# A re-planned start of a matmul kernel: load order, weight pieces and early next tiles

## The chip, the cores and the metric

The kernel runs on one core of a Trainium2 chip. Times are device microseconds of a whole execution. A profile shows one execution; its span, from the first to the last instruction, lies some 2 us under that execution's time (387.9 against 389.72 us for the kernel before).

## The reference

```python
# x: (8, 1024, 768) f32, w_qkv: (768, 2304) f32, out: (8, 1024, 2304) f32
rms = np.sqrt(np.mean(x ** 2, axis=-1, keepdims=True) + eps)
return np.matmul(x / rms * gamma, w_qkv)
```

## The kernel before

The 8,192 rows make 64 tiles of 128. A tile is converted to bf16, transposed (K onto the partitions), multiplied with the weights (six K blocks, columns in chunks of 512 and a last 256), scaled by 1/rms while the results are copied out of PSUM, the memory that TensorE writes to (an eviction), and stored. Gamma is multiplied into the weights as they are converted. Each engine runs its instructions in the order in which the plan lists them, and SyncE issues nearly all DMAs, also in that order.

Six tiles, the head, are planned by hand while the 7.1 MB of weights arrive. Each entry of the list has a planned time, which only sorts it; tiles 0 to 2 are transposed on TensorE in f32 in two parts (`trA`, `trB`), tiles 3 to 5 in bf16 (`tr`), all later ones by DMA.

```python
ARRIVALS = "xxxwwwxwwwwwxxwww"          # order of the first loads
PIECES = [(0, 1, 0, 512), (1, 2, 0, 512), ...]   # K blocks from, to; column, columns
HEAD_PLAN = [(4.41, "trA", 0), ..., (8.02, "mm", 0, 0, "0"), ...]   # cut
HEAD_END = 44.51
...
for t in range(HEAD, MT):
    at(now - 15, load_x, t)
    at(now - 8.5, cast, t)
    at(now - 7.5, trans_dma, t)
    at(now - 5, stat, t)
    at(now - 3, recip, t)
    for n0 in range(0, N, NT):
        at(now, mm, t, n0, range(KO))
        now += min(NT, N - n0) * US
        flip ^= 1
        evac_at(now + 0.2, t, n0, "DVE" if flip else "ACT", gap=1.2)   # and store
for _, _, fn, args in sorted(plan, key=lambda p: p[:2]):
    fn(*args)
```

Of the kernel before, what the change touches and what calls it, by code (L numbers as in the profile page):

```python
# [7 lines left out]



ARRIVALS = "xxxwwwxwwwwwxxwww"
PIECES = [(0, 1, 0, 512), (1, 2, 0, 512), (2, 3, 0, 512), (3, 4, 0, 512), (4, 5, 0, 512), (5, 6, 0, 512), (0, 3, 512, 512), (3, 6, 512, 512), (0, 6, 1024, 512), (0, 6, 1536, 512), (0, 6, 2048, 256)]

EARLY = 3


HEAD_PLAN = [
    (4.41, "trA", 0), (4.45, "stat", 0), (5.28, "trB", 0), (5.42, "cpA", 0, "DVE"),
    (5.71, "trA", 1), (5.85, "cpB", 0, "ACT"), (6.10, "recip", 0), (6.44, "stat", 2),
    (6.59, "trB", 1), (6.73, "cpA", 1, "DVE"), (6.80, "trA", 2), (7.11, "conv", 0, 0, "POOL"),  # L20
    (7.24, "trB", 2), (7.41, "cpB", 1, "DVE"), (7.77, "cpA", 2, "ACT"),
    (7.81, "conv", 1, 1, "DVE"), (8.02, "mm", 0, 0, "0"), (8.23, "mm", 1, 0, "0"),
    (8.29, "recip", 2), (8.39, "cpB", 2, "ACT"), (8.45, "conv", 2, 2, "DVE"),
    (8.45, "mm", 2, 0, "0"), (8.66, "mm", 0, 0, "1"), (8.75, "stat", 1), (8.88, "mm", 1, 0, "1"),
    (9.10, "mm", 2, 0, "1"), (9.31, "mm", 0, 0, "2"), (9.44, "cast", 3, "DVE"),
    (9.53, "mm", 1, 0, "2"), (9.74, "mm", 2, 0, "2"), (10.05, "tr", 3), (10.08, "stat", 3),
    (10.11, "conv", 3, 3, "DVE"), (10.59, "recip", 1), (10.65, "mm", 0, 0, "3"),
    (10.78, "conv", 4, 4, "DVE"), (10.87, "mm", 1, 0, "3"), (11.09, "mm", 2, 0, "3"),
    (11.26, "cp", 3, "DVE"), (11.32, "mm", 0, 0, "4"), (11.45, "conv", 5, 5, "ACT"),
    (11.54, "mm", 1, 0, "4"), (11.76, "mm", 2, 0, "4"), (11.82, "recip", 3),  # L30
    (11.97, "mm", 3, 0, "01234"), (13.05, "mm", 0, 0, "5"), (13.27, "mm", 1, 0, "5"),
    (13.47, "conv", 6, 0, "DVE"), (13.47, "conv", 6, 1, "ACT"), (13.47, "conv", 6, 2, "POOL"),
    (13.48, "mm", 2, 0, "5"), (13.70, "mm", 3, 0, "5"), (13.95, "evac", 2, 0, "DVE"),
    (14.01, "mm", 0, 512, "0"), (14.18, "evac", 0, 0, "ACT"), (14.22, "mm", 1, 512, "0"),
    (14.44, "mm", 0, 512, "12"), (14.70, "evac", 1, 0, "DVE"), (14.87, "evac", 3, 0, "ACT"),
    (14.87, "mm", 1, 512, "12"), (15.30, "mm", 2, 512, "012"), (15.48, "conv", 7, 4, "DVE"),
    (15.48, "conv", 7, 5, "POOL"), (15.95, "mm", 3, 512, "012"), (16.33, "conv", 7, 3, "POOL"),
    (16.47, "cast", 4, "DVE"), (16.47, "stat", 4), (16.60, "mm", 0, 512, "45"),
    (17.03, "mm", 1, 512, "4"), (17.24, "tr", 4), (17.47, "cast", 5, "DVE"),
    (17.58, "mm", 0, 512, "3"), (17.79, "mm", 1, 512, "35"), (17.80, "stat", 5),  # L40
    (18.02, "cp", 4, "DVE"), (18.23, "tr", 5), (18.56, "mm", 2, 512, "345"), (18.58, "recip", 4),
    (18.74, "evac", 1, 512, "DVE"), (19.13, "evac", 0, 512, "ACT"), (19.21, "mm", 3, 512, "345"),
    (19.49, "evac", 2, 512, "DVE"), (19.86, "mm", 4, 0, "012345"), (20.02, "evac", 3, 512, "ACT"),
    (20.24, "recip", 5), (20.40, "cp", 5, "DVE"), (21.15, "mm", 4, 512, "012345"),
    (21.49, "conv", 8, 2, "DVE"), (21.49, "conv", 8, 3, "ACT"), (21.97, "conv", 8, 0, "DVE"),
    (22.20, "conv", 8, 4, "ACT"), (22.45, "mm", 5, 0, "012345"), (22.45, "evac", 4, 0, "DVE"),
    (22.91, "evac", 4, 512, "ACT"), (23.60, "conv", 8, 1, "ACT"), (23.74, "mm", 5, 512, "012345"),
    (23.90, "evac", 5, 0, "DVE"), (24.31, "conv", 8, 5, "ACT"), (25.04, "mm", 0, 1024, "012345"),
    (25.20, "evac", 5, 512, "DVE"), (25.51, "conv", 9, 0, "POOL"), (25.51, "conv", 9, 1, "ACT"),
    (25.95, "conv", 9, 5, "DVE"), (26.33, "mm", 1, 1024, "012345"), (26.43, "conv", 9, 4, "DVE"),  # L50
    (26.49, "evac", 0, 1024, "ACT"), (26.91, "conv", 9, 2, "DVE"), (27.39, "conv", 9, 3, "DVE"),
    (27.63, "mm", 2, 1024, "012345"), (27.87, "evac", 1, 1024, "DVE"),
    (27.90, "conv", 10, 0, "POOL"), (27.90, "conv", 10, 2, "ACT"), (28.38, "conv", 10, 3, "ACT"),
    (28.62, "conv", 10, 5, "DVE"), (28.86, "conv", 10, 4, "ACT"), (28.92, "conv", 10, 1, "DVE"),
    (28.92, "mm", 3, 1024, "012345"), (29.22, "evac", 2, 1024, "DVE"),
    (30.22, "mm", 4, 1024, "012345"), (30.38, "evac", 3, 1024, "DVE"),
    (31.51, "mm", 5, 1024, "012345"), (31.67, "evac", 4, 1024, "DVE"),
    (32.81, "mm", 0, 1536, "012345"), (32.97, "evac", 5, 1024, "DVE"),
    (34.10, "mm", 1, 1536, "012345"), (34.26, "evac", 0, 1536, "DVE"),
    (35.39, "mm", 2, 1536, "012345"), (35.55, "evac", 1, 1536, "DVE"),  # L60
    (36.69, "mm", 3, 1536, "012345"), (36.85, "evac", 2, 1536, "DVE"),
    (37.98, "mm", 4, 1536, "012345"), (38.14, "evac", 3, 1536, "DVE"),
    (39.28, "mm", 5, 1536, "012345"), (39.44, "evac", 4, 1536, "DVE"),
    (40.57, "mm", 0, 2048, "012345"), (40.73, "evac", 5, 1536, "DVE"),
    (41.23, "mm", 1, 2048, "012345"), (41.39, "evac", 0, 2048, "ACT"),
    (41.88, "mm", 2, 2048, "012345"), (42.04, "evac", 1, 2048, "DVE"),
    (42.54, "mm", 3, 2048, "012345"), (42.70, "evac", 2, 2048, "DVE"),
    (43.19, "mm", 4, 2048, "012345"), (43.35, "evac", 3, 2048, "DVE"),
    (43.85, "mm", 5, 2048, "012345"), (44.01, "evac", 4, 2048, "DVE"),
    (44.67, "evac", 5, 2048, "DVE"),  # L70
]
HEAD_END = 44.51


@with_exitstack
def kernel(
# [20 lines left out]
    KO = K // P  # L97
    MT = M // P
    NT = 512
    HEAD = ARRIVALS.count("x")  # L100
    inv_k = 1.0 / float(K)
    PIECE_BUFS = {(k1 - k0, n): sum((q[1] - q[0], q[3]) == (k1 - k0, n) for q in PIECES)
                  for k0, k1, _, n in PIECES}

    PARTS = [(0, 1024), (1024, 1024), (2048, N - 2048)]

    singles = ctx.enter_context(tc.tile_pool(name="singles", bufs=1))
    wst = ctx.enter_context(tc.tile_pool(name="wst", bufs=3))
    xin = ctx.enter_context(tc.tile_pool(name="xin", bufs=8))
    stats = ctx.enter_context(tc.tile_pool(name="stats", bufs=12))  # L110
    junk = ctx.enter_context(tc.tile_pool(name="junk", bufs=2))
    xbp = ctx.enter_context(tc.tile_pool(name="xbp", bufs=4))
    xTp = ctx.enter_context(tc.tile_pool(name="xTp", bufs=HEAD + 3))
    outp = ctx.enter_context(tc.tile_pool(name="outp", bufs=7))
    psum = ctx.enter_context(tc.tile_pool(name="psum", bufs=8, space=bass.MemoryType.PSUM))

# [25 lines left out]
    def load_w(c):  # L142
        k0, k1, n0, n = PIECES[c]
        WF[c] = wst.tile([P, k1 - k0, n], f32, name=f"w_f{k1 - k0}_{n}", bufs=PIECE_BUFS[k1 - k0, n])
# [56 lines left out]
            XT[t] = xTp.tile([P, KO, P], bf16, name="xT")  # L201
        copy(eng, XT[t][:, slice(*HALF[h]), :], PT[t, h])

    def trans_dma(t):
        XT[t] = xTp.tile([P, KO, P], bf16, name="xT")
        nc.sync.dma_start_transpose(out=XT[t], in_=XB[t])

# [34 lines left out]
    def at(time, fn, *args):  # L242
        plan.append((time, len(plan), fn, args))
# [21 lines left out]
            nc.tensor.matmul(out=wps, lhsT=warm, rhs=warm, start=True, stop=True)  # L265


    nx = nw = 0
    for n, kind in enumerate(ARRIVALS):
        if kind == "x":  # L270
            at(0.1 * n - 9, load_x, nx)
            nx += 1
        else:
            at(0.1 * n - 9, load_w, nw)
            nw += 1
    at(0.0, idle, 30)
    ops = {"conv": conv, "cast": cast, "stat": stat, "recip": recip, "tr": tr, "cp": cp, "mm": mm}
    for time, op, *args in HEAD_PLAN:
        if op == "evac":
            evac_at(time, *args, gap=1.0)  # L280
        elif op[-1] in "AB":
            at(time, tr_half if op[:2] == "tr" else cp_half, args[0], op[-1], *args[1:])
        else:
            if op == "mm":
                args[2] = [int(k) for k in args[2]]
            at(time, ops[op], *args)
        if op == "trA" and args[0] == 0:
            at(time + 0.1, gamma_in)
        if op == "trB" and args[0] == EARLY - 1:
            at(time + 0.1, idle, 5)  # L290


    US = 6 * 0.2158 / 512
    now, flip = HEAD_END, 0
    for t in range(HEAD, MT):
        at(now - 15, load_x, t)
        at(now - 8.5, cast, t)
        at(now - 7.5, trans_dma, t)
        at(now - 5, stat, t)
        at(now - 3, recip, t)  # L300
        for n0 in range(0, N, NT):
# [3 lines that stand above are left out]
            evac_at(now + 0.2, t, n0, "DVE" if flip else "ACT", gap=1.2)  # L305
# [38 lines left out]
```

## Time and profile before

| | before |
|---|---|
| time, median | 389.93 us (389.67 to 390.10, 3 runs) |
| TensorE busy | 379.5 of 387.9 us |
| first product matmul | 8.48 us |
| tile 7's first matmul | 51.56 us, after a wait of 0.44 us |
| last eviction starts | 384.37 us |
| from there to the end (the tail) | 3.5 us |

TensorE is the limit from 8.5 us on.

### The profile page before, as it was taken

How to read it: one execution, taken by the hardware profiler on the slowest of the kernel's cores; microseconds unless marked ns; L12 is line 12 of the kernel's file. 1: busy time of each engine (PE TensorE's matmuls, PEld its weight loads, DVE VectorE, ACT ScalarE, POOL GpSimd, SP SyncE). 2: the span in 40 equal slices, each digit the busy share in tenths (PEclk: the TensorE clock that was granted, in tenths of full speed). 3: DMA queues.
4: the chain of work that ended last, by engine and by line, in shares of the span. 5: the costliest groups of instructions: out<-in, count | busy, mean ns of one | idle time of the engine just before them, and what ended most of it. 6: DMA issues, size and time to landing. Idle time of an engine off the chain costs nothing.

```text
span 387.9 us, 5500 instructions
## 1 busy us (share of the span) xinstructions
PE 379.5 (98%) x1953; PEld 194.3 (50%) x1992; DVE 159.1 (41%) x317; ACT 178.1 (46%) x359; POOL 5.9 (2%) x12
## 2 busy tenths in 40 slices
PE   7999999999999999999999999999999999999996
PEld 6444644554554554554554554554554554554553
DVE  3667634343433343433343433343334343334332
ACT  6652234544444544444534444534434535434532
POOL 1310000000000000000000000000000000000000
PEclk9999999999999999999999999999999999999999
DMA  7999999999999999999999999999999999999974
GB/s 272 392 384 358 308 369 284 397 301 274 333 311 305 279 326 295 290 330 300 276 346 288 302 317 280 318 311 304 287 318 301 297 318 303 287 325 292 292 264 189
DMA packets 87606, 119.51 MB, mean 308 GB/s; under 512 B 50710, under 2 KB 59676, under 8 KB 87580
## 3 DMA queue, kind: packets, MB, share of 16 engines
q1 hardware_dynamic: 87568, 119.17, 100.7%
q8 instruction: 15, 0.25, 0.3%
q14 instruction: 11, 0.09, 0.1%
q10 hardware_dynamic: 12, 0.00, 0.0%
HBM read 32.25 MB, written 75.50 MB: 278 GB/s over the span
## 4 chain that ended last, share of the span: by engine, by line
PE 94%; DMA 3%; SPq 1%; issue 1%; DVE 0%; ACT 0%
PE pm L216 94%; DMA w_f<-in_w_qkv_dram 2%; DMA xT<-xb 2%; SPq L140 0%; SPq L145 0%; PE pm L183 0%; DVE w_b L151 0%; ACT ot L232 0%; DVE ot L230 0%
## 5 line engine op out<-in xcount | busy, mean ns | idle before, releaser
L216 PE MATMUL pm<-w_b,xT 128*128 128x512 bf16 (+1 forms) x1881 | 372.4, 357 | 3.0 <-DMA xT<-xb 0.4
L216 PEld LDWEIGHTS <-xT 128*128 128x128 bf16 x1920 | 187.6, 98 | 186.6 <-issue 0.8
L230 DVE TENSOR_SCALAR ot<-pm,rstd 128x512 f32<-128x512 f32 (+1 forms) x168 | 116.7, 696 | 210.3 <-PE pm L216 210.3
L232 ACT ACTIVATE ot<-pm,rstd 128x512 f32<-128x512 f32 (+1 forms) x152 | 97.9, 645 | 187.0 <-PE pm L216 141.7
L170 ACT ACTIVATE sq<-x_t 128x768 bf16<-128x768 f32 x64 | 53.4, 834 | 10.2 <-DMA x_t<-in_x_dram 10.2
L159 DVE CAST xb<-x_t 128x768 bf16<-128x768 f32 x61 | 33.2, 545 | 4.1 <-DMA x_t<-in_x_dram 4.0
L172 ACT ACTIVATE rms<-ssq,eps_sb 128x1 f32<-128x1 f32 x64 | 18.8, 294 | 2.1
L170 ACT ACTIVATION_READ_ACCUMULATOR sq<-x_t 128x1 f32 x64 | 12.2, 191 | 0.0
L177 DVE RECIPROCAL rstd<-rms 128x1 f32<-128x1 f32 x64 | 9.8, 153 | 0.0
L151 DVE TENSOR_SCALAR w_b<-w_f,g_sb 128x512 bf16<-128x512 f32 (+1 forms) x14 | 6.5, 494 | 6.1 <-DMA w_f<-in_w_qkv_dram 6.0
L153 ACT ACTIVATE w_b<-w_f,g_sb 128x512 bf16<-128x512 f32 (+1 forms) x10 | 6.1, 651 | 5.7 <-DMA w_f<-in_w_qkv_dram 5.7
L155 POOL TENSOR_SCALAR w_b<-w_f,g_sb 128x512 bf16<-128x512 f32 (+1 forms) x6 | 5.2, 864 | 23.5 <-DMA w_f<-in_w_qkv_dram 23.5
L265 PE MATMUL pm<-warm 128*128 128x128 bf16 x35 | 3.8, 300 | 1.0 <-DVE eps_sb L124 1.0
L265 PEld LDWEIGHTS <-warm 128*128 128x128 bf16 x35 | 3.5, 142 | 1.0 <-DVE eps_sb L124 1.0
L197 PE MATMUL pm<-ident_f,x_t 128*128 128x128 f32 x18 | 2.8, 292 | 0.8 <-DMA x_t<-in_x_dram 0.8
L197 PEld LDWEIGHTS pm<-ident_f,x_t 128*128 128x128 f32 x18 | 2.2, 155 | 1.1 <-DMA x_t<-in_x_dram 1.0
L127 ACT ACT_TABLE_LOAD x1 | 1.3, 1283 | 1.3 <-PEq L325 1.3
L159 DVE CAST xT<-pm 128x512 bf16<-128x512 f32 (+1 forms) x3 | 1.7, 596 | 0.0
L159 DVE COPY xT<-pm 128x768 bf16<-128x768 bf16 x3 | 1.6, 547 | 0.0
L248 DVE COPY g_sb<-pm 128x6 f32<-128x6 f32 x1 | 0.2, 165 | 3.6 <-PE pm L247 3.6
L183 PEld LDWEIGHTS <-xb 128*128 128x128 bf16 x18 | 1.2, 98 | 0.9 <-DVE xb L159 0.6
L183 PE MATMUL pm<-ident,xb 128*128 128x128 bf16 x18 | 1.5, 220 | 0.0
(13 smaller groups left out, 3.1 us busy)
## 6 DMA issues: line engine op xcount, KB each, us to landing
out_dram<-ot SPq DMA_DIRECT2D x126, 512.0 KB, 4.0
x_t<-in_x_dram SPq DMA_DIRECT2D x64, 384.0 KB, 4.3
out_dram<-ot SPq DMA_DIRECT2D x64, 128.0 KB, 3.2
w_f<-in_w_qkv_dram SPq DMA_DIRECT2D x2, 1536.0 KB, 13.3
w_f<-in_w_qkv_dram SPq DMA_DIRECT2D x3, 768.0 KB, 8.5
w_f<-in_w_qkv_dram SPq DMA_DIRECT2D x6, 256.0 KB, 5.8
out_dram<-ot SPq DMA_DIRECT2D x4, 256.0 KB, 2.0
xT<-xb SPq DMA_TRANSPOSE x58, 4.4
```

The lines of the kernel that those rows point to most:

```text
L151: nc.vector.tensor_scalar(out=o, in0=i, scalar1=g, scalar2=None, op0=mult)
L153: nc.scalar.activation(out=o, in_=i, func=AF.Copy, scale=g, bias=0.0)
L155: nc.gpsimd.tensor_scalar(out=o, in0=i, scalar1=g, scalar2=1.0, op0=mult, op1=mult)
L159: nc.vector.tensor_copy(out=out, in_=in_)
L170: nc.scalar.activation(out=sq, in_=X[t], func=AF.Square, accum_out=ssq)
L172: nc.scalar.activation(out=rms, in_=ssq, func=AF.Sqrt, scale=inv_k, bias=eps_sb)
L177: nc.vector.reciprocal(out=r, in_=RS[t])
L197: nc.tensor.transpose(out=PT[t, h][:, ko - k0, :], in_=X[t][:, ko * P:(ko + 1) * P], identity=ident_f)
L216: nc.tensor.matmul(out=PM[t, n0][:, :nl], lhsT=XT[t][:, ko, :], rhs=w_b[:, ko, n0:n0 + nl], start=(b == 1), stop=(b == KO))
L230: nc.vector.tensor_scalar(out=o, in0=pm[:, :nl], scalar1=RS[t], scalar2=None, op0=mult)
L232: nc.scalar.activation(out=o, in_=pm[:, :nl], func=AF.Copy, scale=RS[t], bias=0.0)
L265: nc.tensor.matmul(out=wps, lhsT=warm, rhs=warm, start=True, stop=True)
```

## The change

The intent is to start with more work per arrived byte, to cut later weights finer, and to have the next tiles' loads and transposes out before the stores crowd SyncE and the DMA rings (the queues of waiting transfers).

```diff
-ARRIVALS = "xxxwwwxwwwwwxxwww"
+LOADS: w0 x0 x1 x2 w1 w2 w3 x3 w4 w5 x4 w6 w7 x5 w8 ... w13 x6 x7     (cut)
-PIECES: 6 single K blocks, 2 of three, then whole column chunks       (cut)
+PIECES: (0,2,0,512), 4 single, 6 pairs, 2 of three, 1 whole chunk     (cut)
-HEAD_PLAN, HEAD_END = 44.51
+HEAD_PLAN (new order, cut), HEAD_END = 44.64
-xin bufs=8, xbp bufs=4, xTp bufs=HEAD + 3, all weight pieces at once
+xin bufs=10, xbp bufs=6, xTp bufs=HEAD + 5, at most 4 of a weight shape
-    at(0.0, idle, 30)            # warm-up matmuls; 5 more later
+    at(0.0, idle, 18)            # then gamma, 28 more; 3 more later
+    at(2.8, gamma_in)
+    at(2.81, idle, 28)
 for t in range(HEAD, MT):
+    ahead = 6.0 if t < HEAD + 5 else 0.0
-    at(now - 15, load_x, t)
-    at(now - 8.5, cast, t)
-    at(now - 7.5, trans_dma, t)
+    if ("x", t) not in {q[1:] for q in LOADS}:
+        at(now - 15 - ahead, load_x, t)
+    at(now - 8.5 - ahead, cast, t)
+    at(now - 7.5 - ahead, xbar, t)
```

## The prediction

> **What bounds the kernel now.** I read the page first (busy shares, slices), then the waits, then the engines in five stretches, then the timeline of the two places where TensorE stood still. The page says that TensorE is busy in 98% of the span, in every slice but the first and the last, and that DMA is full in nearly all of them too.
>
> ```profile
> PE 379.5 (98%) x1953; PEld 194.3 (50%) x1992; DVE 159.1 (41%) x317; ACT 178.1 (46%) x359; POOL 5.9 (2%) x12
> ...
> PE   7999999999999999999999999999999999999996
> ...
> PEclk9999999999999999999999999999999999999999
> DMA  7999999999999999999999999999999999999974
> ```
>
> The waits of TensorE on others, all that exceed the list's threshold (engine, line, what it waited for, total us, times, longest), are tiny, and all lie in the first 52 us:
>
> ```profile
> PE pm L265 <- DVE eps_sb L124: 1.0, 1, 1.0
> PE pm L197 <- DMA x_t<-in_x_dram: 0.8, 1, 0.8
> PE pm L216 <- DMA xT<-xb: 0.4, 1, 0.4
> PE pm L216 <- POOL w_b L155: 0.4, 1, 0.4
> PE pm L216 <- DVE w_b L151: 0.2, 1, 0.2
> ```
>
> The stretches split the span at the first real matmul (8.48 us), the first matmul of tile 6 (45.33, the end of the hand-ordered head), the first of tile 7 (51.56) and the last matmul (384.37):
>
> ```profile
> 8.48:45.33 36.85, 36.48 (x195) 18.63 (x199) 25.35 (x51) 17.46 (x37) 4.47 (x5) 1.00 1.04 357
> 45.33:51.56 6.23, 5.74 (x29) 2.72 (x28) 2.92 (x6) 1.74 (x3) 0.00 (x0) 1.00 1.05 390
> 51.56:384.37 332.81, 330.98 (x1676) 167.24 (x1710) 128.39 (x254) 153.80 (x310) 0.00 (x0) 1.00 1.02 304
> ```
>
> The last row is 57 tiles in 332.81 us, 5.839 us each. A tile is 13,824 columns of matmul, so 512 columns cost 5.839 / 27 = 0.2163 us. The span is then 8.48 lead-in + 36.85 head + 6.23 tile 6 + 332.81 steady + 3.53 tail (last eviction and store) = 387.90. Only three terms can shrink without fewer matmuls. The head's six tiles are 162 x 0.2163 = 35.04 us of matmul, so it loses 36.85 - 35.04 = 1.81 us; tile 6 loses 6.23 - 5.84 = 0.39 us; and 8.48 us pass before any product. The steady 86% of the span is not touched by the change.
>
> The head's loss is seen in the timeline of TensorE (start, length, engine, line, operation, idle before it):
>
> ```profile
> 8.48 2.10 PE L216 MATMUL pm<-w_b,xT 128*128 128x512 bf16 x8 [0.39 <-POOL w_b L155]
> 10.52 0.51 PE L183 MATMUL pm<-ident,xb 128*128 128x128 bf16 x6
> 11.19 6.80 PE L216 MATMUL pm<-w_b,xT 128*128 128x512 bf16 x30 [0.15 <-DVE w_b L151]
> 17.82 0.50 PE L183 MATMUL pm<-ident,xb 128*128 128x128 bf16 x6
> ```
>
> Three bf16 transposes of six at 0.34 us in the chain are 1.0 us; the other 0.8 us is waiting for weights between 8.5 and 14.6. After 19.3 the head runs at the full rate: from there 120 of the 162 units remain, 26.0 us, which gives 45.3, as observed. Tile 6's loss comes from tile 7's transposed input:
>
> ```profile
> 45.48 1.39 SPq L206 DMA_TRANSPOSE xT<-xb  x1
> ...
> 51.56 10.76 PE L216 MATMUL pm<-w_b,xT 128*128 128x512 bf16 x51 [0.44 <-DMA xT<-xb]
> ```
>
> It was issued at 45.48, behind stores that wait on SyncE for evictions, and landed 6.0 us later, 0.44 us too late.
>
> **What the Trainium skill says.** "TensorE: Matmul & The Clock Gate", section "Wait — 56ns, not 53.3ns?", gives 215.7 ns start to start for warm 512-column matmuls; the 216.3 ns above agree, so the steady part is at its floor. Part 1 of the same page says that the array runs at half clock until some 3.4 us of sustained activity; the trace's 30 warm-up matmuls took 3.38 us, 0.113 us each, near the half rate, though the granted clock reads 1.00 there. "DMA: Bandwidth & Descriptors", section "Anatomy of one DMA", says that a semaphore wait of a DMA happens on the issuing sequencer before dispatch; the row at 45.48 agrees, since the transpose's input was cast by 42.7 and the issue came 2.8 us later. The same page's section "Queues, rings and completion order" says that each DMA engine takes descriptors in ring order; so what stands early in SyncE's list lands early, which is what the change uses.
>
> **The change, part by part.**
>
> *Loads and first matmuls.* Before, the order is x0 x1 x2, then six single K blocks of weights; after, two K blocks in one piece (0.52 MB), x0 x1 x2, four single blocks. From the trace I read when loads landed against MB in the list: x2 (1.18 MB) at 6.92, first weights (1.44) at 7.74, then 8.32 (1.70), 8.90 (1.97), x3 (2.36) at 9.90, 10.64 (2.62), 12.06 (3.15), 14.03 (3.93), 18.03 (5.51): from 1.18 MB on, 4.33 MB in 11.1 us, 0.39 MB/us. The changed list has x0 at 0.92 MB, x1 at 1.31, x2 at 1.70: read off the same curve, about 6.1, 7.3 and 8.3. The new plan's own times have 5.95, 7.0 and 7.9, so up to 0.4 earlier than my curve; the old plan was 0.46 early at its first matmul (8.02 planned, 8.48 in the trace). In the changed instruction order the first half transpose of x2 stands ahead of the first matmul on TensorE. Four f32 transposes take about 0.6 us (18 have a mean start-to-start of some 0.15), so the first matmul comes between 8.4 (plan) and 8.95 (8.33 + 0.6): call it 8.7, **0.2 later** than before. In return two K blocks per tile are ready then: 6 x 0.216 = 1.3 us of work instead of 0.65, so the next blocks (landing at 8.9, 9.6, 10.3 by the curve, plus 0.5 to 1.0 for the conversion) should be ready in time. The lost 0.8 us of weight waits should fall to about 0.3. The second half transpose of x2, 0.3 us, now stands between real matmuls. The three later PE transposes stay: 1.0 us. Head end: 8.7 + 35.04 + 1.0 + 0.3 + 0.3 = 45.3; with the plan's landings, 44.64 plus some 0.2 of unmodelled gaps = 44.85. I take **45.1**, a gain of 0.2.
>
> *Weights in thirds and halves.* By 0.39 MB/us they land at about 13.4, 15.7, 17.0, 19.4, 20.6, and the matmuls that need them are planned at 14.1, 17.9, 20.4 and, for the third column block, 25.2. Only the first has less than 1 us of slack. Conversions are the same 36 K blocks on three engines, so no engine gains work: DVE and ACT are at 69% and 47% of the head (25.35 and 17.46 of 36.85). After 19 us the weights were no limit before, and finer pieces can't win there.
>
> *Next tiles ahead of stores.* Loads of tiles 6 and 7 move ahead of the first store, casts and transposes of tiles 6 to 10 come 6 us earlier. The plan puts the transposes of 6 and 7 at about 31 and 37 instead of 37 and 43. Even behind the whole backlog (10.2 MB of loads and six 0.52 MB stores are 13.4 MB, at 0.39 from about 3 us done by 37) tile 6 lands near 38 and tile 7 in the low 40s, 6 us or more ahead of 45.1 and 50.9. This takes out the **0.4 us** of tile 6. No other tile waited, so the rest of the head start buys nothing.
>
> *Warm-ups.* 46 instead of 35 matmuls, all before the first x is there: 18 until about 3.0, gamma's transpose, 28 until about 6. Free, unless x0 comes earlier.
>
> Sum: 0.2 + 0.4 = 0.6 us of span, so 387.3, and 389.93 - 0.6 = **389.3 us**.
>
> **The rivals.** (1) *Late x2 holds back everything:* 0.9 MB more per first operand; if x2 lands at 8.5 and the piece for the second column block at 13.7, the first matmul is at 9.1 and the head ends at 45.7. That eats the 0.4: 389.9, no change. For it: bandwidth in the trace dips to about 220 GB/s at 5 to 6 us, where the first weights move, and now they move first; against it: the plan was rebuilt with later landings. (2) *The plan holds, and the old waits all vanish:* head end 44.6, tile 6 without loss: 0.7 + 0.4 = 1.1 us, 388.8. For it: the list has the same number of matmuls and a fuller start. (3) *A wait takes the place of the one removed:* DVE's cast of tile 6 stands ahead of the evictions of the third column block, and a late x6 would hold PSUM; or stores pushed back hold output buffers. Eight PSUM tiles with six in use give some 3 us of slack, and seven output buffers some 40 us, so I give it little: if so, 390.5. No path leads to 2% (7.8 us), since all losses together that lie within the change's reach are 2.2 us plus the lead-in.
>
> **Range and chances.** Executions before lie within 0.45 us. Rivals 1 and 2 span 388.8 to 389.9; I widen by a few tenths for run scatter: 388.6 to 390.0. Faster by over 2%: 0.4%; within 2%: 99.2%; slower by over 2%: 0.4%.
>
> **What would show it.** Right: the first matmul with weights at 8.4 to 9.0; no idle of a weight wait over 0.2 us after it; tile 6's first matmul at 44.8 to 45.4; no wait of TensorE on a transposed tile at all; then 58 tiles at 5.84 and a tail of 3.5. Wrong: a first matmul after 9.2, a wait for weights near 14 us, a steady tile that isn't 5.84, or a new wait of TensorE on an eviction (PSUM) between 30 and 45 us.

## The result and the profile after

| | before | after |
|---|---|---|
| time, median of 4 runs | 390.01 (389.67 to 390.19) | 389.50 (389.32 to 389.81) |
| span of the profiled run | 387.9 | 387.6 |
| first product matmul | 8.48 | 8.53 |
| tile 7's first matmul | 51.56 | 50.69 |
| last eviction starts | 384.37 | 383.49 |
| from there to the end | 3.5 | 4.1 |

The ratio of times is 0.9989, with a 95% interval of 0.9971 to 1.0006: the same within 2%, and from these four runs alone not even surely faster. A ratio is the mean time of one kernel's fast runs over that of the other's in the same rounds, so it isn't quite the ratio of the medians quoted. A second job with six runs (below) gave 0.9984 (0.9972 to 0.9997).

The waits of TensorE in the changed kernel, the whole list (total us, times, longest):

```profile
PE pm L280 <- DVE eps_sb L139: 1.0, 1, 1.0
```

Only the start is left. Neither weights nor a transposed tile is waited for. TensorE's timeline in the head (start, length, engine, line, operation, count):

```profile
6.03 1.84 PE L212 MATMUL pm<-ident_f,x_t 128*128 128x128 f32 x12
7.71 0.33 PE L280 MATMUL pm<-warm 128*128 128x128 bf16 x3
8.07 0.63 PE L212 MATMUL pm<-ident_f,x_t 128*128 128x128 f32 x4
8.53 1.03 PE L231 MATMUL pm<-w_b,xT 128*128 128x512 bf16 x4
9.40 0.38 PE L212 MATMUL pm<-ident_f,x_t 128*128 128x128 f32 x2
9.61 2.32 PE L231 MATMUL pm<-w_b,xT 128*128 128x512 bf16 x10
11.77 0.50 PE L198 MATMUL pm<-ident,xb 128*128 128x128 bf16 x6
...
19.77 40.58 PE L231 MATMUL pm<-w_b,xT 128*128 128x512 bf16 x211
```

x2's transposes start at 8.07 and there is no idle time behind them. (Lengths reach into the next line because a matmul's modelled end overlaps the next one's start.) The same three stretches as before, at the changed kernel's own borders: head, tile 6, the other 57 tiles (length, then busy us of PE, that is TensorE, of its weight loads, of VectorE, ScalarE and GpSimd, then granted clock, DMA share, GB/s):

```profile
8.53:44.86 36.33, 36.33 (x203) 18.72 (x201) 23.88 (x51) 19.61 (x39) 3.90 (x6) 1.00 1.06 361
44.86:50.69 5.83, 5.83 (x32) 2.94 (x30) 2.55 (x6) 1.14 (x2) 0.00 (x0) 1.00 1.02 413
50.69:383.45 332.76, 332.76 (x1712) 167.22 (x1709) 128.17 (x253) 154.51 (x311) 0.00 (x0) 1.00 1.03 304
```

The steady part is unchanged (332.76 against 332.81). Tile 7 starts 0.87 us earlier, and so does the last eviction, 0.88 us. Of the 0.87, 0.44 is the wait on tile 7's transpose; the remaining 0.43 is the head. The first matmul of the kernel before moves by up to 1.0 us between traces of that head (below), and this trace of it is the earliest, so the pair of traces is no mean of what the head brings. The transposes of tiles 6 and 7, which the kernel before issued at 38.37 and 45.48, now go out here (SyncE's timeline):

```profile
30.98 1.72 SPq L221 DMA_TRANSPOSE xT<-xb  x1
...
34.17 1.92 SPq L221 DMA_TRANSPOSE xT<-xb  x1
```

They landed at 40.8 and 42.5, some 4 and 8 us ahead of their use.

So TensorE is done 0.88 us earlier, but the span is only 0.3 us shorter: the tail took back 0.6 us. The last eviction ends the chain of waits in both kernels (start, length); first the kernel before, then the changed one:

```profile
384.37 0.47 ACT ot L232
```

```profile
383.49 0.47 ACT ot L247
```

SyncE's last two stores, again before and after:

```profile
384.50 0.81 SPq L236 DMA_DIRECT2D out_dram<-ot  x2
```

```profile
383.61 1.09 SPq L251 DMA_DIRECT2D out_dram<-ot  x2
```

In the kernel before the second store goes out at 384.92, 0.07 us after its eviction has ended. In the changed kernel the eviction ends at 383.96 and the store goes out at 384.37: SyncE did nothing for 0.36 us. I had not expected that.

A reading trap: the group of product matmuls has all 1,920 records in the first trace after, and 1,881 in the second one of the same kernel.

```profile
L231 PE MATMUL pm<-w_b,xT 128*128 128x512 bf16 (+1 forms) x1920 | 374.3, 358 | 0.0
```

```profile
L231 PE MATMUL pm<-w_b,xT 128*128 128x512 bf16 (+1 forms) x1881 | 372.2, 357 | 2.1
```

Where 39 records are missing, the chain shows "issue" holes of 0.05 us every 49 matmuls and TensorE seems 2 us idle; a steady tile takes 5.835 us in both.

### The profile page after: what moved, and what is told of

Its sections match the earlier page's. It is cut to its first block, busy times and chain, and to the rows that moved or that the text cites. A ratio compares the mean times of both kernels' runs of the same rounds, so it can differ in the third digit from the quotient of the medians.

```text
span 387.6 us, 5580 instructions
## 1 busy us (share of the span) xinstructions
PE 382.3 (99%) x2006; PEld 195.7 (50%) x2006; DVE 157.2 (41%) x316; ACT 180.4 (47%) x360; POOL 4.6 (1%) x12
## 4 chain that ended last, share of the span: by engine, by line
PE 97%; DMA 1%; SPq 0%; ACT 0%; issue 0%
PE pm L231 96%; DMA x_t<-in_x_dram 1%; PE pm L212 0%; PE pm L198 0%; ACT ot L247 0%; SPq L155 0%; SPq L160 0%; PE pm L280 0%
## 5 line engine op out<-in xcount | busy, mean ns | idle before, releaser
L245 DVE TENSOR_SCALAR ot<-pm,rstd 128x512 f32<-128x512 f32 (+1 forms) x164 | 113.4, 693 | 214.0 <-PE pm L231 213.7
L247 ACT ACTIVATE ot<-pm,rstd 128x512 f32<-128x512 f32 (+1 forms) x156 | 101.1, 648 | 191.9 <-PE pm L231 146.1
L280 PE MATMUL pm<-warm 128*128 128x128 bf16 x49 | 5.4, 299 | 1.0 <-DVE eps_sb L139 1.0
L280 PEld LDWEIGHTS <-warm 128*128 128x128 bf16 x49 | 4.9, 141 | 1.0 <-DVE eps_sb L139 1.0
L170 POOL TENSOR_SCALAR w_b<-w_f,g_sb 128x512 bf16<-128x512 f32 (+1 forms) x6 | 3.9, 653 | 25.1 <-DMA w_f<-in_w_qkv_dram 25.1
L174 DVE CAST xT<-pm 128x256 bf16<-128x256 f32 (+1 forms) x5 | 2.7, 531 | 1.6 <-PE pm L212 1.3
```

Source lines behind the costliest of these rows:

```text
L170: nc.gpsimd.tensor_scalar(out=o, in0=i, scalar1=g, scalar2=1.0, op0=mult, op1=mult)
L174: nc.vector.tensor_copy(out=out, in_=in_)
L245: nc.vector.tensor_scalar(out=o, in0=pm[:, :nl], scalar1=RS[t], scalar2=None, op0=mult)
L247: nc.scalar.activation(out=o, in_=pm[:, :nl], func=AF.Copy, scale=RS[t], bias=0.0)
L280: nc.tensor.matmul(out=wps, lhsT=warm, rhs=warm, start=True, stop=True)
```

## The experiments

Three questions: which part of the change gives the 0.9 us on TensorE's path, what makes the tail longer, and whether the load order is the reason that the head starts well. Tail here is last eviction's start to the end of the span. "Before" is the kernel before in the same job; medians in us.

| run | time | before | ratio, 95% interval | first matmul | last eviction | tail |
|---|---|---|---|---|---|---|
| e1 before again | 389.80 | 390.04 | 0.9994 (0.998 to 1.0009) | 8.88 | 384.56 | 3.5 |
| e2 after again | 389.52 | 390.04 | 0.9984 (0.9972 to 0.9997) | 8.52 | 383.38 | 4.1 |
| e3 head only | 391.80 | 390.04 | 1.0046 (1.0029 to 1.0062) | 8.53 | 386.03 | 4.1 |
| e4 next tiles ahead only | 389.23 | 390.04 | 0.9978 (0.9964 to 0.9993) | 8.67 | 383.91 | 3.5 |
| e5 after, one store split | 388.96 | 389.90 | 0.9978 (0.9964 to 0.9991) | 8.55 | 383.61 | 3.6 |
| e6 before, five stores split | 391.09 | 389.90 | 1.0033 (1.002 to 1.0045) | 9.48 | 385.24 | 4.2 |
| e7 x first | 390.11 | 389.90 | 1.0008 (0.9996 to 1.0021) | 9.51 | 384.16 | 4.2 |
| e8 x first, one store split | 389.79 | 389.90 | 1.0003 (0.999 to 1.0015) | 10.07 | 384.72 | 3.6 |
| e9 before, early touch | 389.90 | 390.05 | 0.9998 (0.9985 to 1.0011) | 8.98 | 384.61 | 3.7 |
| e10 e8 and early touch | 389.67 | 390.05 | 0.9992 (0.9979 to 1.0005) | 9.76 | 384.42 | 3.5 |
| e11 e5, first matmuls earlier | 388.83 | 390.05 | 0.9972 (0.996 to 0.9984) | 7.57 | 383.44 | 3.6 |
| e12 loads ahead, transposes not | 390.12 | 390.12 | 1.0 (0.9987 to 1.0014) | 8.71 | 384.46 | 3.6 |

### Both kernels again (e1, e2): no edit

> The kernel before, unchanged, against itself. Both theories: ratio 1.000 within 0.001; its trace shows the last matmul near 384.1 us, the wait of tile 7 on its transposed input near 51 us (0.3 to 0.6 us) and a tail of about 3.6 us from the last matmul's end to the span's end. If tail or stall differ by 0.3 us or more from the first trace, differences of that size between single traces mean nothing.

> The changed kernel again. Theory (gain on the TensorE path is 0.9 us, 0.6 us of it lost again in the tail): ratio 0.9985 to 0.999 (0.4 to 0.6 us faster), last matmul near 383.2, tail near 4.2 us again. Rival (the longer tail of the one trace is chance): tail near 3.6 us, span near 387.0.

The theory held: the last evictions are 1.2 us apart here and the tails 3.5 and 4.1 us, as in the first pair. The longer tail is not chance. The first matmul of the kernel before moves by 0.4 us between these traces (8.48 and 8.88), that of the changed one by 0.01. With the later traces of unchanged heads it is 8.48 to 9.48 for the old head (five traces) and 8.52 to 8.71 for the new one (five, without e11).

### The two parts apart (e3, e4)

e3 is the changed kernel with the old timing and buffers of the next tiles:

```diff
-    (-8.80, "x", 6), (-8.79, "x", 7),
-        ahead = 6.0 if t < HEAD + 5 else 0.0
+        ahead = 0.0
-xin bufs=10, xbp bufs=6, xTp bufs=HEAD + 5
+xin bufs=8, xbp bufs=4, xTp bufs=HEAD + 3
```

> The changed kernel with its new head, but with the loads, casts and transposes of tiles 6 to 10 at the old times and behind the stores, and the old buffer counts. Theory (both parts matter, and the second sets when tile 7 can start): tile 6 starts 0.3 us earlier than before, but tile 7 waits longer for its transposed input (0.6 to 1.0 us), the last matmul stays within 0.3 us of the kernel before, and with the changed kernel's longer tail the time is the same or up to 0.6 us slower than before. Rival (the new head alone brings the gain): 0.3 to 0.5 us faster than before.

e4 is the kernel before with the new timing and buffers of the next tiles:

```diff
+    at(-7.3, load_x, HEAD)
+    at(-7.2, load_x, HEAD + 1)
-        at(now - 15, load_x, t)
-        at(now - 8.5, cast, t)
-        at(now - 7.5, trans_dma, t)
+        ahead = 6.0 if t < HEAD + 5 else 0.0
+        if t > HEAD + 1:
+            at(now - 15 - ahead, load_x, t)
+        at(now - 8.5 - ahead, cast, t)
+        at(now - 7.5 - ahead, trans_dma, t)
```

> The kernel before with its old head, but tiles 6 and 7 loaded ahead of all stores, casts and transposes of tiles 6 to 10 six us earlier, and the new buffer counts. Theory: no wait of tile 7, last matmul 0.5 to 0.6 us earlier than before, tail 3.6 us as before, so 0.5 to 0.6 us faster than before: as fast as the whole change, within 0.2 us. Rival (the new head brings the gain): under 0.2 us faster.

The new head alone is 1.8 us slower than before; I had expected at most 0.6. TensorE's waits and timeline in e3:

```profile
PE pm L230 <- DMA xT<-xb: 2.1, 3, 1.1
```

```profile
51.24 6.01 PE L230 MATMUL pm<-w_b,xT 128*128 128x512 bf16 x29 [0.48 <-DMA xT<-xb]
58.38 1.90 PE L230 MATMUL pm<-w_b,xT 128*128 128x512 bf16 x8 [1.14 <-DMA xT<-xb]
```

Three tiles wait, not one. Their transposes were issued at 46.44, 52.48 and 58.13, each behind stores, and took 4.8, 5.9 and 6.7 us to land. SyncE between the transposes of tiles 6 and 7, first in the kernel before, then in e3:

```profile
40.43 2.26 SPq L236 DMA_DIRECT2D out_dram<-ot  x3
42.78 1.05 SPq L140 DMA_DIRECT2D x_t<-in_x_dram  x1
43.92 1.46 SPq L236 DMA_DIRECT2D out_dram<-ot  x2
45.48 1.39 SPq L206 DMA_TRANSPOSE xT<-xb  x1
```

```profile
38.88 4.43 SPq L250 DMA_DIRECT2D out_dram<-ot  x5
43.40 1.17 SPq L154 DMA_DIRECT2D x_t<-in_x_dram  x1
44.66 1.69 SPq L250 DMA_DIRECT2D out_dram<-ot  x2
46.44 2.34 SPq L220 DMA_TRANSPOSE xT<-xb  x1
```

In both, 13 stores in all stand ahead of tile 7's transpose, but seven of them instead of five now come after tile 6's: the new plan finishes the fourth column chunk later (its first eviction is planned at 37.63 instead of 34.26). So the transpose goes out 1.0 us later, while TensorE needs it 0.4 us earlier. That this bunching is the cause is read from the traces; moving the stores alone was not tried. With transposes at the old times, at any rate, the new head loses more than it gains: the second part is what the first one needs.

The second part alone is worth all that was measured: 0.8 us in time, no wait on a transposed tile, and tail 3.5 (0.5 to 0.6 was expected; between e4 and the whole change the intervals overlap). On TensorE's path the new head seems to add to it: the last eviction is at 383.91 in e4 and at 383.4 to 383.6 in the four traces with the new head and with the next tiles ahead (after, e2, e5, e11). From the first matmul to the last eviction e4 takes 375.24 us and after, e2 and e5 374.86 to 375.06, so 0.2 to 0.4 us of the difference do not come from the start; but e4 is one trace. It paid for that with the longer tail.

### What in "next tiles ahead" matters (e12)

e12 is e5 (below) with early loads but casts and transposes at their old times:

```diff
-        at(now - 8.5 - ahead, cast, t)
-        at(now - 7.5 - ahead, xbar, t)
+        at(now - 8.5, cast, t)
+        at(now - 7.5, xbar, t)
```

> The changed kernel with the split store of tile 20, with x loads early and ahead of the stores as in the change, but casts and transposes of tiles 6 to 10 at their old times. It tells apart which half of 'next tiles ahead of stores' takes tile 7's wait away. Theory (the transpose stands behind the stores on SyncE and in the DMA rings, however early its input is there): tile 7's transpose is issued near 45 us and lands near 51, so TensorE waits 0.5 to 1.0 us at tile 7, perhaps at tile 8 too, and the last matmul is 0.7 to 2.6 us later than with the split store alone (383.3). Rival (the late load was the cause; early loads are enough): no wait, last matmul near 383.2.

The theory held, though tile 8 is the one that shows it: tile 7's transpose went out at 46.55 and landed at 50.80, just in time but for some 0.2 us, and tile 8's went out at 52.26, in TensorE's timeline:

```profile
57.49 4.71 PE L231 MATMUL pm<-w_b,xT 128*128 128x512 bf16 x21 [0.64 <-DMA xT<-xb]
```

The last eviction is 0.86 us later than in e5, 0.16 of it from a later first matmul. The medians differ by 1.2 us, but on two chips; by the ratios to the kernel before it is 0.9 us. Early inputs are not enough: the transposes (moved here together with the casts) must be ahead of the stores.

### The tail (e5, e6)

In the traces SyncE pauses at the same places of its own record count, 78, 206, 334, 462 and 590, whatever it has to do then: 128 records apart. With no other wait in the way a pause takes 0.34 to 0.39 us, the first one 0.44 to 0.46; from record 16 on no other place has a pause in all fourteen traces. In the kernel before, record 590 lies behind the last store: the pause is not gone but falls among the closing waits (387.21 to 387.59). With three more DMAs and their waits (602 records instead of 593) it lies between the last store's wait and the store. e5 moves it by one split store in the changed kernel, e6 puts it between the last two stores of the kernel before:

```diff
+        elif left[t, h] == 0 and h == 0 and t == 20:        # e6: 20 <= t < 25
+            at(time + gap, store, t, h, PARTS[h][0], 512)
+            at(time + gap, store, t, h, PARTS[h][0] + 512, 512)
         elif left[t, h] == 0:
             at(time + gap, store, t, h, *PARTS[h])
```

> The changed kernel with one more SyncE DMA in mid run: the first store of tile 20 in two halves of 512 columns. SyncE then has two more instructions ahead of its last store. In all six traces so far SyncE pauses 0.34 to 0.46 us each 128 of its instructions (78, 206, 334, 462, 590 of its records), and in the changed kernel and in the head alone the last pause falls just ahead of the last store. Theory (that pause makes the longer tail): it now falls where SyncE waits for an eviction anyway; tail 3.6 to 3.8 us instead of 4.2, last matmul at 383.1 as before, 0.35 to 0.6 us faster than the changed kernel. Rival (the tail is longer for another reason, such as what lies in the DMA queues): tail 4.1 to 4.2 us, same time as the changed kernel.

> The kernel before with five such split stores (tiles 20 to 24), which puts the pause between its last two stores. Theory: tail 3.9 to 4.2 us instead of 3.6, last matmul unchanged near 384.1, 0.3 to 0.6 us slower than before. Rival: tail 3.6 us, same time.

SyncE's last two stores, e5 first, then e6:

```profile
383.73 0.81 SPq L251 DMA_DIRECT2D out_dram<-ot  x2
```

```profile
385.37 1.08 SPq L236 DMA_DIRECT2D out_dram<-ot  x2
```

The two issues take 0.81 us where the pause is elsewhere, and 1.08 or 1.09 where it falls among them, in both kernels. The tail follows: 3.6 in e5, 4.2 in e6, and again 4.2 in e7 and 3.6 in e8 (below), which differ by the split store alone. Over all fourteen traces the five with the pause there (after, e2, e3, e6, e7) have tails of 4.1 to 4.2, and the nine others 3.5 to 3.7. Between before and after, the last store leaves 0.33 us later behind its eviction, takes 0.21 longer to land, and the closing waits 0.06 longer: that is the 0.6. Why the landing is longer was not tested. e5's five runs, 388.81 to 389.29, all lie at or under the fastest of ten of the changed kernel (389.29), though on another chip; by the ratios to the kernel before (0.9978 and 0.9984) the difference in time is not resolved.

e6 lost 1.2 us, more than the 0.7 that the tail explains. In its trace, which is of its slowest run, x2 landed at 7.83 against 6.89 in the first trace before, so TensorE began 1.0 us later; why, with an unchanged head, stays open. From the first matmul to the last eviction it takes no longer than before (375.76 against 375.89 us), so the split stores cost nothing there.

### The order of the first loads (e7, e8, e9, e10)

e7 loads the three x tiles ahead of the first pair of K blocks and transposes them while the pair arrives:

```diff
-LOADS: w0 x0 x1 x2 w1 ...
+LOADS: x0 x1 x2 w0 w1 ...
-    at(2.81, idle, 28)
+    at(2.81, idle, 8)
-HEAD_PLAN up to 9.9: conv 0, trA/trB of tiles 0 to 2 among the first matmuls (cut)
+HEAD_PLAN: trA, trB of tiles 0 to 2, 20 warm-ups, conv 0, then six matmuls in a row (cut)
```

> The changed kernel with the three x tiles loaded ahead of the first two K blocks, all three transposed while the weights arrive, 20 warm-ups fewer early and 17 more later; everything from the third K block on as it was. If bytes per time alone decide (the same 1.7 MB by the first pair of K blocks, landing near 7.9), the first matmul is at 8.5 as before, but the 0.85 us of f32 transposes are behind TensorE then instead of between its matmuls: tile 6 starts 0.2 to 0.5 us earlier, tail 4.2, total 0.2 to 0.5 us faster than the changed kernel. Rival (the loading of x is slowed where the first weights follow, as in the kernel before, where x2 landed 2.0 us after x1 and the first weights at 7.6): first matmul at 8.8 or later, no gain.

> x first and the split store of tile 20 together: the two gains add if they are independent, so 0.6 to 1.0 us faster than the changed kernel, near 388.6; if x first gives nothing, as the split store alone.

The rival was right. The first matmuls came at 9.51 and 10.07 instead of 8.53. In e7's timeline of TensorE:

```profile
7.30 0.85 PE L214 MATMUL pm<-ident_f,x_t 128*128 128x128 f32 x6 [0.69 <-DMA x_t<-in_x_dram]
...
9.51 3.20 PE L233 MATMUL pm<-w_b,xT 128*128 128x512 bf16 x14 [0.79 <-DVE w_b L168]
```

The same 1.70 MB were complete at 8.83 with x first and at 7.93 with weights first. This is not one pair's chance: over all fourteen traces it is 8.22 to 9.24 in the eight with x first (the kernel before and e1, e4, e6 and e9 among them) and 7.78 to 8.11 in the six with weights first. The rates of the first 12 us, in 40 slices of 0.3 us, of the changed kernel and then of e7:

```profile
GB/s 0 0 0 0 0 5 160 125 177 198 225 321 335 393 437 437 389 410 369 430 348 406 420 389 413 389 430 382 410 393 430 369 420 372 386 396 396 375 403 382
```

```profile
GB/s 0 0 0 0 0 70 92 154 329 410 379 348 420 389 256 246 266 253 219 311 311 348 348 314 382 355 372 386 376 427 379 413 417 396 369 369 348 362 396 375
```

With weights first the slow stretch is one with the start; with x first there is a second one, from 4.2 to 7 us. Single packets of it took up to 1.2 us, where the median is 0.084 for 2 KB and 0.121 for 3 KB. My explanation was that first reads of the weights are slow; e9 (the kernel before) and e10 (e8) were to test it by a small read of them at the very start:

```diff
+    touch = singles.tile([P, 16], f32)
+    nc.scalar.dma_start(out=touch, in_=w_qkv[0:P, 0:16])
```

> The kernel before with one small extra load at the very start: the first 16 columns of the first K block of the weights (128 rows of 64 bytes), issued on ScalarE's queue right after gamma, into a tile that nothing reads. In all traces with x first, x2 landed 1.6 to 2.9 us after x1 and DMA moved little at 4 to 6.5 us, with single 2 or 3 KB packets that took about 1 us where the median takes 0.1; with weights first, such packets are at 1.5 to 3 us and x2 lands at 7.8 to 7.9 every time. Theory (the first reads of the weights are slow, whenever they come): after the small load the slow packets are at 1.5 to 3 us too, x2 lands at 6.0 to 6.5, the first matmul moves from 8.5 to 7.7 to 8.1, and the last matmul is 0.3 to 0.6 us earlier than before. Rival (it is the change from x to weights in the stream, or something else at that time): x2 still lands at 6.8 or later and nothing is gained.

> x first, the split store of tile 20, and the small early load of weights. Theory of slow first reads: x2 lands near 6.2 and the pair of K blocks near 7.8, first matmul near 8.5 instead of 9.5 to 10, tile 6 starts near 44.4, 0.8 to 1.4 us faster than x first with the split store alone, and 0.2 to 0.6 us faster than the changed kernel with the split store. Rival: as x first with the split store, near 389.8.

The rates in e9 sag from 3.9 us on as they did:

```profile
GB/s 0 0 0 0 0 82 164 256 430 358 420 329 415 250 181 195 276 253 157 201 321 348 362 413 382 331 362 376 447 369 406 427 376 389 396 410 396 416 396 389
```

x2 landed at 7.43 and 7.42 in e9 and e10, and the time did not change clear of noise. But the test was not the one intended: the small read, issued at 1.32, moved nothing before 3.4 us. ScalarE's queue in e9 from 0 to 3.4 us (12 packets of gamma) and from 3.4 to 4.5 (the 128 of the small read, and 16 more):

```profile
q10 hardware_dynamic: 12, 0.00, 0.4%
```

```profile
q10 hardware_dynamic: 144, 0.01, 8.8%
```

So e9 and e10 do not decide. What speaks against the explanation is in the packets of e7: seven slow ones (over 0.4 us), all of x, start from 4.14 to 4.73 us, and the first packet of weights starts at 5.11. In all eight traces with x first at least one slow packet of x, after 3.2 us, comes ahead of the first weights. The order of the loads matters; what makes the second slow stretch is open.

### Filling the last hole (e11)

```diff
-    (7.26, "idle", 3),
-    (8.37, "mm", 0, 0, "01"),
+    (7.935, "mm", 0, 0, "01"),
```

with e5's split store.

> The changed kernel with the split store of tile 20, and with tile 0's first two matmuls moved ahead of x2's first transposes on TensorE, in place of three warm-ups. They need x0 alone and can run while x2 is still on its way. If the work ahead of the head's end is what counts, tile 6 starts 0.1 to 0.3 us earlier, and the time is 0.1 to 0.3 us under the changed kernel with the split store; if x2's copies then hold the second and third tile, no gain.

The first matmul is at 7.57, but x2 still lands at 7.94 and the last eviction is at 383.44, inside the spread of e5 and the changed kernel (383.4 to 383.6). The 0.1 us between e11 and e5 is not resolved, and an earlier first matmul alone gained nothing on TensorE's path. Against the kernel before it is the best ratio measured, 0.9972, and its slowest run but one is under the changed kernel's fastest on the same chip (389.07 against 389.29). e4, e5 and e11 all have lower medians than either kernel.

## Why the prediction was right

The time (389.3 forecast, 389.50 measured) and the size of the gain (0.6 and 0.5 us) held, but one term of the sum was mis-sized and another not in it, and they nearly cancel. That the total came out so close is in part luck: the gain on TensorE's path was 0.88 us, not 0.6, and the tail took 0.6 back.

- **Floor and steady part:** right. 58 tiles at 5.84 us, all within 0.05 us in sum.
- **The wait of tile 7 (0.4):** right in size, and e4 and e12 show its cause as told. Its role was larger than told: without this part the new head costs 1.8 us (e3). The prediction said that the rest of the head start "buys nothing"; e12's tile 8 and e3's three tiles show that it is needed with the new head. And the row at 45.48 shows no wait of its own: the transpose's input was ready at 42.7, and it followed the store before it on SyncE by 0.1 us.
- **The head (0.2):** mis-sized, it was 0.43. By the curve the head was to end at 45.3, by the plan at 44.85; 45.1 was a middle, and it ended at 44.86. Two terms made the difference. The first matmul came at 8.53 instead of 8.7. The step that failed there is "read off the same curve": it put x2 at 8.3, and it landed at 7.93, where the plan had it (and from its four transposes' start to the first matmul it was 0.46 us, not 0.6). And the waits for weights fell to 0, not 0.3: the next K blocks landed at 8.62, 9.30 and 9.96, some 0.3 earlier than read. The curve had been taken with x first, and bytes against time is not one curve: the order changes it by 0.3 us at 1.70 MB between before and after, and by 0.9 between e7 and after. So the first rival, late x2, had the wrong sign.
- **The tail (3.5):** wrong, 4.1. "Then 58 tiles and a tail of 3.5" took the tail as untouched, since the stores of the last tile are. Its cause is the place of SyncE's pause, which three more DMAs and their waits moved to just ahead of the last store (e5, e6).
- **The third rival**, PSUM or output buffers taking the place of the wait: no such wait is in the trace. **The finer pieces:** no wait for weights is left; what the pieces, the load order and the new plan each brought to the head was not tried apart.
- **Small slips:** the landings listed for weights are starts of the first reader, up to 0.2 us after the landing (8.22, not 8.32, at 1.70 MB). The conversions are 30 K blocks in both kernels, not 36. The warm-ups are 49, not 46, and the last three run at 7.71, after x0. None of this changes the sum by more than 0.1 us. Loads did land in list order, as the argument from ring order needs (5.01, 5.97, 6.95, 7.93, 8.62 in the changed kernel).

## What to carry to other kernels

When a kernel is at its floor in the middle, add up the start, the first hand-over and the tail, and check each of them after a change, also those that the change doesn't touch. In a head that keeps DMA full, put the next tiles' transposes ahead of the stores before you re-plan anything else: otherwise a new order can bunch the stores in front of them (e3 lost 1.8 us). Measure landings in the order that you will use: the curve from another order was off by 0.4 us here, and orders differed by up to 0.9. Before a test is read, look whether its edit did in the trace what it was meant to do (e9).

## What the Trainium skill lacked or had wrong

- "Runtime: NRT & Kernel Launch", section "Instruction fetch mechanics", gives instruction blocks of 16 KiB, 256 instructions, and calls the cost of crossing one mostly hidden. Here SyncE pauses each 128 of its records, for 0.34 to 0.39 us where nothing else holds it (0.44 to 0.46 at the first), and a pause just ahead of the last store goes with a tail of 4.1 to 4.2 instead of 3.5 to 3.7 us. The traces hold packets of kind "instruction": of 16,384 bytes on queue 8 and of 8,192 on queue 14. In all fourteen, one of 8,192 follows 1.0 to 1.4 us after SyncE's fifth pause begins; in the changed kernel at 385.30. At the page's 64 bytes an instruction (16 KiB are 256) that is 128 instructions, as many as lie between two pauses. That the fetch makes the pause is argued from this and from the even spacing, and not shown.
- "DMA: Bandwidth & Descriptors" has no word on a slow stretch after the start: with x first, single packets took up to 1.2 us at 4 to 7 us (e7) against medians of 0.08 and 0.12, and the same 1.70 MB took 0.9 us longer than with weights first. The cause is open.
- "Advanced Engine Details and Errata", section "X-Bar Transpose (TRN2)", calls transposes as fast as plain DMAs, and the traces agree: from issue to landing the median is 4.4 us, and 4.2 for the loads of x (after, 60 to 380 us). What it lacks is the time behind queued stores, 4.8 to 6.7 us for a tile's transpose in e3, which a plan must budget for.
- No page tells how missing matmul records read in a trace: in the second trace of the changed kernel 1,881 of 1,920 are there, and TensorE seems 2 us idle.
